# Down projection of 16 of the 22 f tiles as block products with sums in HBM, and the FFN in the order of a list scheduler

## The chip, the cores and the metric

The kernel runs on one core of one Trainium2 chip. A core has a matrix engine (PE in the profile), a vector engine (DVE), a scalar engine (ACT), GpSimd (POOL) and SyncE (SP), and 16 DMA engines that move data between HBM and the on-chip memory SBUF. The matrix engine adds up into PSUM, which this kernel uses as 8 banks of 128x512 fp32. The metric is the device time of one launch in microseconds (us), lower is better.

## The reference

One hybrid decoder layer on 1024 tokens of width 1024, in fp32: a mixer (attention and short convolution), then a gated ConvFFN. The change touches the FFN alone:

```python
h = rms_norm(x, norm_ffn_pre[l])
u = causal_dwconv(h @ w_up[l], conv_ffn_w[l])
a, g = jnp.split(u, 2, axis=-1)
f = (jax.nn.gelu(g, approximate=True) * a) @ w_down[l]
x = x + rms_norm(f, norm_ffn_post[l])
```

`w_up` is 1024 x 5632, `w_down` is 2816 x 1024. The 2816 FFN channels are 22 f tiles of 128 channels.

## The kernel before

**Numbers.** Every fp32 operand of a matmul is scaled by a power of two and split into two f16 tensors, hi and lo: ACT writes hi (L97), DVE writes lo as the rest (L98). A product is then three f16 matmuls, hi by hi, hi by lo and lo by hi (`PASSES`). The power of two comes from the sum of squares of the operand: ACT squares a tile and sums (L58), PE adds over partitions (L76), DVE builds the scale. All matmuls of the FFN put 512 columns through the array.

**Up projection.** For each f tile the channels a and g are computed as a 2x2 block product with seven products instead of eight (Strassen's scheme): class `Up`, `prod` (L1594), 12 matmuls a product, 84 an f tile. The products are evicted by ACT (L1609) or DVE (additions), then each of a and g goes through a three-tap convolution (one ACT pass L1669, two DVE passes L1671), g through gelu on ACT (L1678), and DVE multiplies (L1679): the result `ua` is an f tile, channels by tokens, 128x1024 fp32. `pair_fetch`, `pair_sums` and `pair_split` load `w_up`, form the sums of weight blocks that the scheme needs and split them.

**Down projection.** The f tiles are taken in groups, `GROUPS = (2, 4, 4, 4, 4, 4)`. `f_split` splits a group's f tiles, `dn_split` loads its `w_down` tiles (L1331) and splits them; `dn_sums` had loaded the same tiles earlier (L1269) for their sums of squares. `down` goes over 8 token tiles of 128 and 2 halves of 512 outputs, each 4 f tiles by 3 passes, 12 matmuls into one bank (L1368). The bank is evicted at once: for the first group by ACT into the accumulator `yacc` (L1373), for the others by DVE, which multiplies by the scale and adds to `yacc` in SBUF (L1375). Per group of four that is 192 matmuls and 16 evictions. The last group also takes the norm of each token row, scales it and sends it out: seven token tiles by a DMA of POOL that adds into `out` in HBM (L1388), the last by SP (L1393).

**Order.** The loop at the end of `ffn` writes the f tiles in turn; the `down` of group g-1 stands in the middle of group g, behind the second f tile's `prod(3)`. Each engine's own order is set by the tile framework's scheduler, from its own priorities. Buffers come from rings: 16 slabs of 128x1024 fp32 (`slot`), 4 for raw weights (`ws`), 8 for split weights (`wh`), 4 and 4 for the accumulators (`o16`, `x`), 8 PSUM banks.

Of the kernel before, what the change touches and what calls it, by code (L numbers as in the profile page):

```python
# [16 lines left out]
F16 = mybir.dt.float16  # L17
# [7 lines left out]
P = 128  # L25
# [9 lines left out]
GROUPS = (2, 4, 4, 4, 4, 4)  # L35
# [4 lines left out]
class Layer:  # L40
# [234 lines left out]
    def mixer(self, mid):  # L275
# [884 lines left out]
        dram = self.top.enter_context(tc.tile_pool(name="dram", bufs=1, space=bass.MemoryType.DRAM))  # L1160
# [112 lines left out]
    dpos, dsums, pz = 0, {}, None  # L1273

# [35 lines left out]
    def ffn(self):  # L1310
# [27 lines left out]
        def down(g, between=None):  # L1338
# [7 lines left out]
            for tt in range(8):  # L1346
                if between:
                    between(tt)
                if g == 0:
                    yacc[tt] = (self.o16p.tile([P, D], F32, tag="o16", name=f"yacc{tt}") if tt < 4 else  # L1350
                                self.xp.tile([P, D], F32, tag="x", name=f"yacc{tt}"))
# [18 lines left out]
                for nh, part in enumerate(parts):  # L1370
                    ps, sl = pd[nh], ds(*part)
                    if g == 0:
                        nc.scalar.activation(y[:, sl], ps, AF.Copy, scale=sm[:, 0:1])  # L1373
                    else:
                        nc.vector.scalar_tensor_tensor(y[:, sl], ps, sm[:, 0:1], y[:, sl], ALU.mult, ALU.add)  # L1375
# [27 lines left out]
        for g in range(ng):  # L1403
            for n in range(GROUPS[g]):
                f = ff0[g] + n
                p = prs[f]
                begun = n == 2 and 1 <= g < ng - 1
                if f >= 1 and not begun:
                    if f >= 2:
                        p.prod(1)  # L1410
                    prs[f - 1].prod(4)
                if f >= 1 and f + 1 < NFF:
                    self.pair_split(f"u{f + 1}")
                if 1 <= f and f + 2 < NFF:
# [309 lines left out]
```

## Time and profile before

| what | us |
|---|---|
| median of 3 runs | 1332.78 (1332.39 to 1333.75) |
| profiled execution, its own time | 1334.14 |
| its span | 1332.4 |
| PE, DVE, ACT, POOL busy in the span | 1313.9, 1049.9, 858.9, 34.4 |
| down projection's matmuls (L1368), 1068 records | 230.3 |

The span runs from the first to the last recorded instruction; the execution's own time is longer by 1.74 us. The FFN takes about the last 650 us of the span, from 682 on. An engine's busy time counts its instructions' own durations; matmuls are pipelined, so a busy PE says only that PE was never without work. Rows by group give a line of the kernel, engine, operation, tiles, shapes and count, then the busy total, the mean of one in ns, and the time for which the engine stood idle just before them and what ended it. Rows by stretch give, for each engine, the busy time in a window, then the clock that TensorE was granted (1.00 is full), the mean busy share of the 16 DMA engines and GB/s.

### The profile page before, as it was taken

How to read it: one execution, taken by the hardware profiler on the slowest of the kernel's cores; microseconds unless marked ns; L12 is line 12 of the kernel's file. 1: busy time of each engine (PE TensorE's matmuls, PEld its weight loads, DVE VectorE, ACT ScalarE, POOL GpSimd, SP SyncE). 2: the span in 40 equal slices, each digit the busy share in tenths (PEclk: the TensorE clock that was granted, in tenths of full speed). 3: DMA queues.
4: the chain of work that ended last, by engine and by line, in shares of the span. 5: the costliest groups of instructions: out<-in, count | busy, mean ns of one | idle time of the engine just before them, and what ended most of it. 6: DMA issues, size and time to landing. Idle time of an engine off the chain costs nothing.

```text
span 1332.4 us, 16830 instructions
## 1 busy us (share of the span) xinstructions
PE 1313.9 (99%) x6505; PEld 590.3 (44%) x6505; DVE 1049.9 (79%) x1701; ACT 858.9 (64%) x1210; POOL 34.4 (3%) x58
## 2 busy tenths in 40 slices
PE   8999999999999999999999999999999999999997
PEld 4444444444444444444444444444444444444443
DVE  6578988887888967877898968966994895798855
ACT  6578878787878966566574877625751762576424
POOL 2000000000000000000110000000000000000002
PEclk9999999999999999999999999999999999999999
DMA  7101210111102112332431113223130321312126
GB/s 270 33 33 33 63 32 32 33 33 32 49 0 67 60 52 91 114 139 63 145 107 34 48 48 127 63 64 121 41 92 26 116 67 46 126 47 111 64 48 111
DMA packets 26610, 96.12 MB, mean 72 GB/s; under 512 B 3089, under 2 KB 3217, under 8 KB 26530
## 3 DMA queue, kind: packets, MB, share of 16 engines
q1 hardware_dynamic: 25088, 89.80, 20.7%
q0 software_dynamic: 1440, 5.24, 2.1%
q8 instruction: 51, 0.84, 0.3%
q14 instruction: 29, 0.24, 0.1%
q10 hardware_dynamic: 2, 0.00, 0.0%
HBM read 86.62 MB, written 8.42 MB: 71 GB/s over the span
## 4 chain that ended last, share of the span: by engine, by line
PE 89%; DVE 6%; ACT 2%; DMA 1%; issue 1%; POOL 0%; SPq 0%; POOLq 0%; DVEq 0%; ACTq 0%
PE pd L1368 16%; PE py L1179 5%; PE pcb L211 3%; PE pcc L211 3%; PE pcx L211 3%; PE pk L211 3%; PE pq L211 3%; PE pywa L805 3%; PE pywc L805 3%; PE A L833 2%; PE o L833 2%; PE z L833 2%; PE pv L406 1%; PE pv L444 1%; PE pga L211 1%
## 5 line engine op out<-in xcount | busy, mean ns | idle before, releaser
L1594 PEld LDWEIGHTS <-wh_u 128*128 128x128 f16 x1848 | 178.8, 98 | 215.1 <-issue 1.2
L1368 PE MATMUL pd<-wdh,f 128*128 128x512 f16 (+1 forms) x1068 | 230.3, 377 | 2.3 <-ACT wdh L97 1.7
L1368 PEld LDWEIGHTS <-f 128*128 128x128 f16 x1068 | 104.4, 98 | 126.5 <-issue 3.6
L97 ACT ACTIVATE wh_u<-ws_u,sc 128x1024 f16<-128x1024 f32 (+1 forms) x66 | 64.7, 999 | 98.3 <-DVE sc L80 79.4
L1375 DVE SCALAR_TENSOR_TENSOR yacc<-pd,sd,yacc 128x512 f32<-128x512 f32 (+1 forms) x81 | 58.6, 741 | 72.7 <-PE pd L1368 65.2
L1594 PEld LDWEIGHTS <-wh_g 128*128 128x128 f16 x588 | 56.9, 98 | 68.6 <-issue 0.2
L1179 PE MATMUL py<-wh_wo,m 128*128 128x512 f16 x384 | 83.7, 379 | 0.0
L98 DVE SCALAR_TENSOR_TENSOR wh_u<-ws_u,sc,wh_u 128x1024 f16<-128x1024 f32 (+1 forms) x66 | 72.2, 1101 | 10.7 <-ACT wh_u L97 10.6
L876 ACT ACTIVATE sh<-sp 128x1024 f16<-128x1024 f32 (+3 forms) x48 | 40.4, 842 | 52.3 <-DVE sp L871 52.1
L1671 DVE SCALAR_TENSOR_TENSOR ugu<-cgu,cw_g,ugu 128x1023 f32<-128x1023 f32 (+1 forms) x44 | 56.3, 1279 | 10.1 <-ACT ugu L1669 9.6
L871 DVE TENSOR_TENSOR sp<-A,sp 1x1024 f32<-1x1024 f32 (+3 forms) x40 | 35.9, 897 | 29.9 <-PE A L833 26.5
L1671 DVE SCALAR_TENSOR_TENSOR ua<-cau,cw_a,ua 128x1023 f32<-128x1023 f32 (+1 forms) x44 | 56.2, 1278 | 1.4 <-ACT ua L1669 1.3
L1179 PEld LDWEIGHTS <-m 128*128 128x128 f16 x384 | 37.4, 98 | 44.2
L880 DVE TENSOR_TENSOR sh<-sp,sh 128x1024 f16<-128x1024 f32 (+3 forms) x48 | 45.8, 954 | 13.5 <-ACT sh L876 13.3
L906 DVE SCALAR_TENSOR_TENSOR w<-e,w 128x1024 f16<-128x1024 f32 (+3 forms) x48 | 45.8, 953 | 6.8 <-ACT w L902 6.7
L902 ACT ACTIVATE w<-e 128x1024 f16<-128x1024 f32 (+3 forms) x48 | 40.5, 843 | 14.8 <-DVE e L897 13.7
L897 DVE TENSOR_TENSOR e<-e,g 128x1024 f32<-128x1024 f32 (+3 forms) x48 | 45.7, 952 | 2.5 <-ACT g L893 2.5
L866 ACT ACTIVATE sp<-e,one 128x1024 f32<-128x1024 f32 (+3 forms) x48 | 44.4, 925 | 4.0 <-DVE e L861 2.7
L58 ACT ACTIVATE jk_u<-ws_u 128x1024 bf16<-128x1024 f32 x44 | 46.4, 1054 | 0.8 <-DMA ws_u<-w_up_nt 0.2
L852 ACT ACTIVATE e<-z,cz 128x1024 f32<-128x1024 f32 (+3 forms) x48 | 43.0, 897 | 3.6 <-PE z L833 3.6
L211 PE MATMUL pcb<-hT,wh_cb 128*128 128x512 f16 x192 | 45.1, 380 | 0.0
L211 PE MATMUL pcx<-hT,wh_cx 128*128 128x512 f16 x192 | 44.9, 379 | 0.0
(711 smaller groups left out, 2625.8 us busy)
## 6 DMA issues: line engine op xcount, KB each, us to landing
ws_u<-w_up_nt SPq DMA_DIRECT2D x44, 512.0 KB
ds<-w_down SPq DMA_DIRECT2D x22, 512.0 KB
wd<-w_down SPq DMA_DIRECT2D x22, 512.0 KB
ws_g<-w_in_nt SPq DMA_DIRECT2D x14, 512.0 KB
x<-x SPq DMA_DIRECT2D x8, 512.0 KB
ws_wo<-w_out SPq DMA_DIRECT2D x8, 512.0 KB
xr<-x SPq DMA_DIRECT2D x8, 512.0 KB
out<-x SPq DMA_DIRECT2D x7, 512.0 KB
```

Source lines behind the costliest of these rows:

```text
L58: self.nc.scalar.activation(self.junk(f"jk_{name}"), src, AF.Square, accum_out=acc)
L97: self.nc.scalar.activation(dst[:, 0, :], src, AF.Copy, scale=s)
L98: self.nc.vector.scalar_tensor_tensor(dst[:, 1, :], src, s, dst[:, 0, :], ALU.mult, ALU.subtract)
L211: nc.tensor.matmul(ps, w[:, wi, ds(k * P, P)], hT[:, hi, k, ds(c * NH, NH)], start=n == 0, stop=n == last)
L805: nc.tensor.matmul(ps, w[0][:, wi, ds((d % 2) * NH + k * P, P)], acts[bi][k][:, hi, ds(c * NH, NH)], start=n == 0, stop=n == 11)
L833: nc.tensor.matmul(out, w, mv, skip_group_check=True, **kw)
L880: nc.vector.tensor_tensor(sh[:, 1, :, off:], u["sp"][:, :, off:], sh[:, 0, :, off:], ALU.subtract)
L1179: nc.tensor.matmul(ps, m16[k][:, hi, ds(tt * P, P)], wo[k][:, wi, sl], start=k == 0 and p == 0, stop=k == 7 and p == 2)
L1368: nc.tensor.matmul(pd[nh], f16[g][k][:, hi, ds(tt * P, P)], w[k][:, wi, ds(*part)], start=run is runs[0] and n == 0, stop=run is runs[-1] ...
L1375: nc.vector.scalar_tensor_tensor(y[:, sl], ps, sm[:, 0:1], y[:, sl], ALU.mult, ALU.add)
L1594: nc.tensor.matmul(ps, w[wt][:, wi, ds(wc * NH + k * P, P)], self.block(i, hi, k), start=first and n == 0, stop=n == 3 * KH - 1, skip_grou ...
L1671: nc.vector.scalar_tensor_tensor(u[:, lag:], c[:, :T - lag], sm[:, 2 - lag:3 - lag], u[:, lag:], ALU.mult, ALU.add)
```

## The change

`GROUPS` becomes (4, 4, 4, 4, 3, 3), and the first `NQ = 4` groups, 16 f tiles, are no longer multiplied as 4 x 16 plain blocks but as "quads". A quad takes its four f tiles as two pairs (x, y) and cuts tokens and outputs in halves, so that each pair is a 2x2 by 2x2 block product, and writes it as seven products `OPS` in the order 1, 2, 5, 3, 7, 4, 6. A product is 4 token tiles by (2 pairs x 3 passes), 24 matmuls; 168 a quad where `down` had 192.

- **Operands.** `f_quads` and `w_quads` form the block sums (`comb`, DVE, 128x512 fp32, 8 for f and 8 for w) and split them: for f and for w each six full splits of 128x1024 and two half ones of 128x512, where four full ones stood for each.
- **Eviction.** After each product ACT scales the bank into a slab tile `st` (28 times a quad, 128x512); two banks fill one tile. Products 2, 3 and 4 go on adding in the banks of 1, 5 and 7 after those were evicted, so the scheme's own sums are partly made in PSUM.
- **Sums in HBM.** Each `st` (512 KB) goes by a DMA of POOL to one of 14 tensors `acc` in HBM: 14 a quad, written plainly by the first quad and added there (`accum_op`) by the other three. At the end of quad 3, `join` builds the eight `yacc` tiles: 20 loads of 256 KB on SP, 8 adding loads of 256 KB on POOL, 12 additions of 128x512 on DVE.
- **The rest.** The last two groups of three f tiles are multiplied by `down` as before, evicted by DVE (16 and 17 evictions). `w_down` is loaded once for quads 1 to 3, twice for quad 0 and for the last six tiles: 32 loads instead of 44. `dn_sums` in the mixer now covers four tiles instead of two.
- **Order.** From the first `prod` after the mixer to the last group, what PE, DVE, ACT, SP and POOL do is registered as jobs of a class `Plan`, with a cost for each kind (the table `C`), a limit on how far ahead of its need a job may run (`AHEAD`), due times (`DUE`) and the sizes of the buffer rings. `Plan.order` runs the list through a model of the engines; the instructions are then written in that order under a manual schedule. PE's matmuls keep the order in which they are written; the other engines take the ready job whose need is nearest. The model lets one DMA after another pass: an `st` has mb=1.6 there, adding or not, a load of 512 KB mb=1.3 (`load`). The tail (`down` of the last two groups) is left to the framework's scheduler.

Lines in the listings of the changed kernel are its own. ACT around the `down` of group 1, before (`f16` and `wdh` are split f and `w_down`, `jk` the squares, `ua` and `ugu` convolution and gelu, `cgu` an eviction of the up projection):

```order
L97 ACTIVATE f16_1_2_7819<-ua4_7356,sc27_7804 128x1024
L97 ACTIVATE f16_1_3_7822<-ua5_7521,sc27_7804 128x1024
L97 ACTIVATE wdh_1_0_7836<-wd2_1_0_7834,sc28_7825 128x1024
L97 ACTIVATE wdh_1_1_7841<-wd2_1_1_7839,sc28_7825 128x1024
L58 ACTIVATE jk_f6_7746,sm_f2_6591<-ua6_7669 128x1024
L1669 ACTIVATE ugu7_7775<-cgu7_7693,cw_g7_7902 128x1024
L97 ACTIVATE wdh_1_2_7846<-wd2_1_2_7844,sc28_7825 128x1024
L97 ACTIVATE wdh_1_3_7851<-wd2_1_3_7849,sc28_7825 128x1024
L1669 ACTIVATE ua7_7867<-cau7_7692,cw_a7_7868 128x1024
L1609 ACTIVATE cgu8_7887<-pu8a_7873 128x512
L1678 ACTIVATE ugu7_7775<-ugu7_7775 128x1024
L58 ACTIVATE jk_f7_7909,sm_f2_6591<-ua7_7867 128x1024
L58 ACTIVATE jk_u10_0_8166,sm_u10_8163<-ws_u10_0_8164 128x1024
L58 ACTIVATE jk_u10_1_8170,sm_u10_8163<-ws_u10_1_8168 128x1024
```

ACT around product 1 of quad 1, after (`fx`, `fs` are split f sums, `wq` split w sums, `st` the evictions of the banks `pq`):

```order
L1462 ACTIVATE fx_1_0_8338<-ua4_7252,sp_f1_8184 128x1024
L1701 ACTIVATE st1_1_0_8370<-pq1_0_1_8322,sd1_8239 128x512
L1701 ACTIVATE st1_1_0_8370<-pq1_1_1_8331,sd1_8239 128x512
L1701 ACTIVATE st1_1_2_8374<-pq1_2_1_8342,sd1_8239 128x512
L1462 ACTIVATE fs_1_0_8378<-ua5_7489,sp_f1_8184 128x1024
L1701 ACTIVATE st1_1_2_8374<-pq1_3_1_8350,sd1_8239 128x512
L59 ACTIVATE jk_f8_8389,sm_f2_6599<-ua8_8193 128x1024
L1462 ACTIVATE fs_1_1_8400<-ua7_8054,sp_f1_8184 128x1024
L1462 ACTIVATE fx_1_1_8411<-ua6_7904,sp_f1_8184 128x1024
L1569 ACTIVATE ua9_8420<-ca9_8258,cw_a9_8030 128x1024
L1569 ACTIVATE ug9_8281<-cg9_8209,cw_g9_8408 128x1024
L1462 ACTIVATE wq_1_5_8432<-ds5_7804,sp_dn1_7882 128x1024
```

The evictions now stand on ACT between splits, convolution passes and gelus, where before it had no eviction of the down projection after the first group.

DVE in the `down` of group 1, before:

```order
L1679 TENSOR_TENSOR ua7_7867<-ugu7_7775,ua7_7867 128x1024
L1375 SCALAR_TENSOR_TENSOR yacc0_7116<-pd1_0_0_7913,sd1_7911,yacc0_7116 128x512
L1375 SCALAR_TENSOR_TENSOR yacc0_7116<-pd1_0_1_7914,sd1_7911,yacc0_7116 128x512
L1375 SCALAR_TENSOR_TENSOR yacc1_7133<-pd1_1_0_7941,sd1_7911,yacc1_7133 128x512
L1375 SCALAR_TENSOR_TENSOR yacc1_7133<-pd1_1_1_7942,sd1_7911,yacc1_7133 128x512
L1668 TENSOR_SCALAR cw_a8_8242<-cfw_91,sc26_7708,g_ffn_5681 128x3
L1375 SCALAR_TENSOR_TENSOR yacc2_7150<-pd1_2_0_7969,sd1_7911,yacc2_7150 128x512
L1375 SCALAR_TENSOR_TENSOR yacc2_7150<-pd1_2_1_7970,sd1_7911,yacc2_7150 128x512
```

DVE ahead of quad 1, after (L1464 is the lo half of a split, L1469 a `comb`, L1543 an eviction of the up projection):

```order
L1571 SCALAR_TENSOR_TENSOR ug8_8124<-cg8_8068,cw_g8_7815,ug8_8124 128x1022
L1469 TENSOR_TENSOR ua5_7489<-ua4_7252,ua5_7489 128x512
L1543 TENSOR_TENSOR cg9_8209<-pu9b_8219,cg9_8209 128x512
L1469 TENSOR_TENSOR ua7_8054<-ua6_7904,ua7_8054 128x512
L1469 TENSOR_TENSOR ua4_7252<-ua4_7252 128x512
L1469 TENSOR_TENSOR ua6_7904<-ua6_7904 128x512
L1469 TENSOR_TENSOR ua4_7252<-ua5_7489,ua4_7252 128x512
L1469 TENSOR_TENSOR ua6_7904<-ua7_8054,ua6_7904 128x512
L1469 TENSOR_TENSOR ua5_7489<-ua5_7489,ua4_7252 128x512
L1469 TENSOR_TENSOR ua7_8054<-ua7_8054,ua6_7904 128x512
```

DVE no longer adds banks to `yacc` there; it makes the block sums of f in place, and the splits of these sums wait for them.

POOL between the mixer and the tail, before:

```order
L182 TENSOR_TENSOR r_post7_6370<-r_post7_6370,neghalf_86 128x1
L182 TENSOR_TENSOR r_ffn7_6433<-r_ffn7_6433,neghalf_86 128x1
L1345 DMA g_ffn_post_11097<-g_ffn_post 128x1024
L182 TENSOR_TENSOR fin0_11100<-fin0_11100,neghalf_86 128x1
L1388 DMA out<-o0_11099 128x1024
```

POOL at the end of quad 3, after (`acc5_0` is product 5's sum for the first two token tiles):

```order
L1428 DMA acc7_0_6615<-st3_7_0_10417 128x1024
L1428 DMA acc7_1_6616<-st3_7_2_10451 128x1024
L1428 DMA acc4_0_6609<-st3_4_0_10507 128x1024
L1428 DMA acc4_1_6610<-st3_4_2_10522 128x1024
L1428 DMA acc6_0_6613<-st3_6_0_10535 128x1024
L1428 DMA acc6_1_6614<-st3_6_2_10559 128x1024
L1428 DMA yacc4_10509<-acc5_0_6611 128x512
L1428 DMA yacc5_10512<-acc5_0_6611 128x512
L1428 DMA u2_0_10262<-acc6_0_6613 128x512
```

Where POOL had nothing to do through the FFN, it now issues the transfers of all quads in turn, and the adding loads of `join` stand behind quad 3's last ones.

```diff
-GROUPS = (2, 4, 4, 4, 4, 4)
+GROUPS = (4, 4, 4, 4, 3, 3)
+NQ = 4
...
                     if last:
                         nc.scalar.activation(self.junk(f"jf{tt}_{nh}")[:, sl], y[:, sl], AF.Square,
                                              accum_out=sm_[:, 3 + nh:4 + nh])
@@ -1400,49 +1396,517 @@
             g = max(g for g in range(ng) if ff0[g] <= f)
             fts[g].append(prs[f].finish(smfs[g][:, f - ff0[g]:f - ff0[g] + 1]))
 
...
-        for g in range(ng):
+        lo, hi = ds(0, NH), ds(NH, NH)
+        pl = Plan(dict(s=16, ws=4, wh=8, o16=4, x=4, pm=8))
+        C = dict(A=0.97, Ah=0.5, Aq=1.18, V=1.21, Vh=0.64, Vp=0.72)
...
+        def load(eng, b, dst, srcf, mb=1.3, r=(), w=None, **kw):
+            e = nc.sync if eng == "SP" else nc.gpsimd
+            j = pl.add(eng, 0.45 if eng == "SP" else 1.1, lambda: e.dma_start(dst(), srcf(), **kw), r,
+                       [b] if w is None else w, ahead=1e9 if kw or r else AHEAD["load"])
...
+        def comb(o, oc, x, xc, y, yc, op, **kw):
+            V(C["Vh"], lambda: vec.tensor_tensor(o.t[:, oc], x.t[:, xc], y.t[:, yc], op),
+              [(x, "l" if xc is lo else "h"), (y, "l" if yc is lo else "h")], [(o, "l" if oc is lo else "h")], **kw)
+
+        AHEAD = dict(load=45.0, sq=40.0, up=32.0, quad=40.0, wq=60.0)
...
+        def f_quads(g):
+            sb = fb[g] = f_scale(g, 1)
+            q = up[f"q{g}"] = Pr()
...
+            q.a11 = slab(f"fa_{g}", [P, 2, T], F16)
+            for p in range(2):
+                halves(q.a11, ds(p * NH, NH), xs[p], lo, sb, n=NH, dreg=f"{p}", sreg="l", ahead=ah)
...
+            for p in range(2):
+                halves(q.ya[p], fall, ys[p], fall, sb, ahead=ah)
+            for p in range(2):
+                x, y = xs[p], ys[p]
+                comb(y, hi, x, hi, y, hi, ALU.add, ahead=ah)
+                comb(x, hi, x, lo, x, hi, ALU.subtract, ahead=ah)
+                comb(x, lo, y, hi, x, lo, ALU.subtract, ahead=ah)
+                comb(y, lo, y, lo, x, lo, ALU.subtract, ahead=ah)
+            for p in range(2):
+                halves(q.ys[p], fall, ys[p], fall, sb, ahead=ah)
+            for p in range(2):
+                halves(q.xs[p], fall, xs[p], fall, sb, ahead=ah)
...
+                load("SP", b, lambda b=b: b.t, lambda n=n: a["w_down"][ff0[g] + n])
+                A(C["Aq"], lambda n=n, b=b: self.sumsq(b.t, sq.t[:, n:n + 1], f"dn{ff0[g] + n}"), [b], [sq], ahead=AHEAD["wq"])
...
+        def w_quads(g):
...
+                sq.tile = self.dsums[g]
+                raw = [slab(f"wr_{g}_{n}") for n in range(4)]
+                for n, b in enumerate(raw):
+                    load("SP", b, lambda b=b: b.t, lambda n=n: a["w_down"][ff0[g] + n])
...
+            for p in range(2):
+                halves(q.b11, ds(p * NH, NH), xs[p], lo, sb, n=NH, dreg=f"{p}", sreg="l", ahead=ah)
+            for p in range(2):
+                halves(q.yb[p], fall, ys[p], fall, sb, ahead=ah)
+            for p in range(2):
+                x, y = xs[p], ys[p]
+                comb(x, lo, x, hi, x, lo, ALU.subtract, ahead=ah)
+                comb(x, hi, y, hi, x, hi, ALU.subtract, ahead=ah)
+                comb(y, hi, y, hi, x, lo, ALU.subtract, ahead=ah)
+                comb(y, lo, y, lo, y, hi, ALU.subtract, ahead=ah)
+            for p in range(2):
+                halves(q.xt[p], fall, xs[p], fall, sb, ahead=ah)
+            for p in range(2):
+                halves(q.yt[p], fall, ys[p], fall, sb, ahead=ah)
...
+        acc, accb = {}, {}
+        for i in range(1, 8):
+            for e in range(2):
+                acc[i, e] = self.dram.tile([P, 2, NH], F32, tag=f"acc{i}_{e}", name=f"acc{i}_{e}")
+                accb[i, e] = note()
+        OPS = {1: ("a11", None, "b11", None), 2: ("ya", 0, "yb", 0), 3: ("ys", 0, "yb", 1), 4: ("ya", 1, "yt", 0),
+               5: ("ys", 1, "xt", 0), 6: ("xs", 0, "yt", 1), 7: ("xs", 1, "xt", 1)}
...
+        def quad_prod(g, i):
+            q, w = up[f"q{g}"], up[f"w{g}"]
+            ft, fc, wt_, wc = OPS[i]
...
+            for tt in range(4):
+                if first:
+                    q.ps[tt] = Buf("pm", lambda tt=tt: self.bank(f"pq{g}_{tt}_{i}"))
...
+                if tt % 2 == 0:
+                    st = slab(f"st{g}_{i}_{tt}", [P, 2, NH])
+
...
+                    for p in range(2):
+                        fo, wo = p if fc is None else fc, p if wc is None else wc
+                        for h, x in PASSES:
+                            pe.matmul(b.t, fa[p].t[:, h, ds(fo * NH + tt * P, P)], wa[p].t[:, x, ds(wo * NH, NH)],
+                                      start=first and n == 0, stop=n == 5, skip_group_check=True)
+                            n += 1
+                pl.add("PE", 1.3, mm, fa + wa, [b], seq=True)
+                A(C["Ah"], lambda tt=tt, b=b, st=st: act.activation(st.t[:, tt % 2, :], b.t, AF.Copy, scale=q.sd.t[:, 0:1]),
+                  [b, q.sd], [(st, str(tt % 2))])
+                if tt % 2:
+                    kw = {} if g == 0 else dict(accum_op=ALU.add)
+                    load("G", None, lambda e=tt // 2: acc[i, e], lambda st=st: st.t, r=[st], w=[accb[i, tt // 2]], mb=1.6, **kw)
...
+        def join(tt):
+            y = yb_[tt] = Buf("o16", lambda: self.o16p.tile([P, D], F32, tag="o16", name=f"yacc{tt}"))
+            z = yb_[tt + 4] = Buf("x", lambda: self.xp.tile([P, D], F32, tag="x", name=f"yacc{tt + 4}"))
+            u = slab(f"u2_{tt}", [P, NH])
+
...
+            def ld(eng, b, sl, reg, i, **kw):
+                load(eng, None, lambda: b.t[:, sl], lambda: m(i), r=[accb[i, tt // 2]], w=[(b, reg)], mb=0.65, **kw)
+            ld("SP", u, slice(0, NH), None, 1)
+            ld("SP", z, lo, "l", 4)
+            ld("SP", z, hi, "h", 7)
+            ld("SP", y, lo, "l", 2)
+            ld("SP", y, hi, "h", 3)
+            ld("G", u, slice(0, NH), None, 6, accum_op=ALU.add)
+            ld("G", z, hi, "h", 5, accum_op=ALU.add)
+            for b, sl, reg in ((y, hi, "h"), (z, lo, "l"), (z, hi, "h")):
+                V(C["Vh"], lambda b=b, sl=sl: vec.tensor_tensor(b.t[:, sl], b.t[:, sl], u.t, ALU.add), [u], [(b, reg)])
...
+            for f in range(NFF):
+                g = max(g for g in range(ng) if ff0[g] <= f)
...
+                if f >= 1 and not (n == 2 and 1 <= g <= NQ):
+                    up_prod(f - 1, 4)
+                    up_done(f - 1)
+                if n == 0 and 1 <= g <= NQ:
+                    f_quads(g - 1)
...
+                if f + 3 < NFF:
+                    up_weights(f + 3)
+                if n == 1 and 1 <= g <= NQ:
+                    quad_open(g - 1)
+                    for k, i in enumerate((1, 2, 5, 3, 7, 4, 6)):
+                        quad_prod(g - 1, i)
+                        if k == 0:
+                            up_prod(f, 4)
+                            up_done(f)
+                if n == 1 and g < NQ:
+                    w_quads(g)
+                if n == 1 and g >= NQ:
+                    w_sums(g)
+                if g == NQ and n == 2:
+                    for tt in range(4):
+                        join(tt)
...
+        while todo:
+            best = None
+            for e, now in eng.items():
+                c = ready[e]
+                if e == "PE" and pos < len(seq) and not seq[pos].n:
+                    c = c + [seq[pos]]
+                pick = None
+                for j in c:
+                    t = max(now, j.t0, j.late - j.ahead)
+                    for b in j.bufs:
+                        if b.pool and not b.begun:
+                            t = max(t, free[b.pool][0] if free[b.pool] else 1e9)
+                    key = (max(t, now + 0.05), j.late - (100 if e == "PE" and not j.seq else 0))
+                    if t < 1e8 and (pick is None or key < pick[0]):
+                        pick = key, t, j
+                if pick and (best is None or pick[1] < best[0]):
+                    best = pick[1], e, pick[2]
...
+            end = t + j.cost
+            eng[e] = end
+            done = end + j.lag
+            if e in ("SP", "G"):
+                dma = max(dma, t + 0.8) + j.load
+                done = max(done, dma + 1.2)
```

More of the change, by code (lines that the diff above doesn't have):

```diff
@@ L1273 @@
     dpos, dsums, pz = 0, {}, None
+    ahead_set, due_set = {}, {}
     def bank(self, name):
@@ L1371, in down @@
                     ps, sl = pd[nh], ds(*part)
[L1372 to L1375, printed above, removed]
+                    nc.vector.scalar_tensor_tensor(y[:, sl], ps, sm[:, 0:1], y[:, sl], ALU.mult, ALU.add)
                     if last:
@@ L1440, in ffn @@
+        self.pw[f"u{NFF - 1}"] = [b.t for b in p.w], pr.inv
         dn_split(ng - 2)
```

347 lines of the change are left out of this document (310 added, 37 removed).

## The prediction

> **What bounds the kernel now.** I read the busy times first, then the chain of work that ended last, both on the page of the kernel before.
>
> ```profile
> span 1332.4 us, 16830 instructions
> PE 1313.9 (99%) x6505; PEld 590.3 (44%) x6505; DVE 1049.9 (79%) x1701; ACT 858.9 (64%) x1210; POOL 34.4 (3%) x58
> PE 89%; DVE 6%; ACT 2%; DMA 1%; issue 1%; POOL 0%; SPq 0%; POOLq 0%; DVEq 0%; ACTq 0%
> ```
>
> PE is busy for 99% of the span and makes 89% of the chain. Next, what PE waits for in the FFN (us in total, times, longest):
>
> ```profile
> PE pd L1368 <- ACT wdh L97: 1.7, 3, 0.8
> PE pt L1197 <- DVE hn L1189: 1.1, 1, 1.1
> PE pu0a L1594 <- ACT cgu L1609: 0.7, 1, 0.7
> PE pd L1368 <- DVE wdh L98: 0.6, 1, 0.6
> ```
>
> Those are all of its waits there, 4.1 us in 650. So matmuls taken away come off the time, as long as nothing else becomes late. How near the others are is told by stretches: a part of the mixer, the first FFN stretch, one group's period each in the third and fourth row, the tail, a dense part of the fourth row's period, and the last wait of the kernel.
>
> ```profile
> 500.00:600.00 100.00, 100.00 (x470) 45.34 (x469) 77.45 (x134) 62.63 (x93) 1.30 (x2) 1.00 0.34 114
> 682.00:793.00 111.00, 108.72 (x515) 49.79 (x513) 93.33 (x152) 74.58 (x111) 3.61 (x4) 1.00 0.18 57
> 906.80:1022.30 115.50, 115.50 (x543) 52.39 (x540) 88.74 (x135) 61.24 (x81) 0.00 (x0) 1.00 0.23 73
> 1137.20:1242.30 105.10, 104.66 (x491) 47.41 (x490) 91.55 (x145) 71.51 (x97) 0.00 (x0) 1.00 0.26 91
> 1242.30:1332.40 90.10, 83.10 (x397) 38.67 (x396) 58.94 (x92) 34.23 (x56) 11.24 (x16) 0.97 0.39 82
> 1170.00:1230.00 60.00, 60.00 (x283) 27.20 (x282) 58.01 (x89) 42.10 (x55) 0.00 (x0) 1.00 0.26 88
> 1324.20:1329.50 5.30, 1.23 (x12) 0.85 (x9) 3.57 (x9) 1.53 (x6) 1.44 (x2) 0.81 0.69 112
> ```
>
> The columns are window, length, then busy time of PE, PEld, DVE, ACT and POOL, the granted clock, the DMA share and GB/s. In a group's period (906.8 to 1022.3) PE never stands, DVE is busy 77%, ACT 53%.
>
> **The sum, PE.** One stretch of the chain prices the matmul:
>
> ```profile
> 883.50 23.31 PE pd L1368 x108
> ```
>
> 23.31 / 108 = 0.2158 us. Each of four quads has 168 matmuls for 192, so 96 fewer: -20.7 us. The last six f tiles keep theirs. That the instructions are really fewer, the order of the built kernel shows; nothing is left of a rival by which the change doesn't do what it says.
>
> **DVE and ACT work of a quad.** The rows, by shape over the whole run, and the plain evictions in one period:
>
> ```profile
> L97 ACT ACTIVATE f<-ua,sc 128x1024 f16<-128x1024 f32 x22 | 23.5, 1134 | 9.3 <-DVE sc L80 9.3
> L98 DVE SCALAR_TENSOR_TENSOR f<-ua,sc,f 128x1024 f16<-128x1024 f32 x22 | 27.5, 1277 | 1.0 <-ACT f L97 1.0
> L97 ACT ACTIVATE wh_u<-ws_u,sc 128x512 f16<-128x512 f32 x22 | 15.7, 714 | 10.0 <-DVE ws_u L1304 9.7
> L98 DVE SCALAR_TENSOR_TENSOR wh_u<-ws_u,sc,wh_u 128x512 f16<-128x512 f32 x22 | 16.4, 745 | 0.1
> L1290 DVE TENSOR_TENSOR s_u<-s_u,ws_u 128x512 f32<-128x512 f32 x22 | 15.1, 686 | 0.2
> L1373 ACT ACTIVATE yacc<-pd,sd 128x512 f32<-128x512 f32 x16 | 10.4, 718 | 5.8 <-PE pd L1368 5.2 <-PE pr L76 0.6
> L1375 DVE SCALAR_TENSOR_TENSOR yacc<-pd,sd,yacc 128x512 f32<-128x512 f32 x16 | 11.5, 748 | 16.5 <-PE pd L1368 14.7 <-PE pr L76 1.8
> ```
>
> For f and w together a quad has 4 full and 4 half splits more, 16 block sums more, 28 evictions on ACT, and loses 16 on DVE.
>
> DVE: 88.74 + 4 x 1.277 + 4 x 0.745 + 16 x 0.686 - 16 x 0.748 = 95.8 us. The period shrinks from 115.5 to 110.3 (24 matmuls), so DVE stands at 87%. ACT: 61.24 + 4 x 1.134 + 4 x 0.714 + 28 x 0.718 = 88.7 us, 80%.
>
> Is that tolerable? The stretch 1137.2 to 1242.3 had DVE at 87% with PE idle for 0.44 us, and in 1170 to 1230 DVE was 97% busy and PE never idle. So load alone is no bound. What counts is waiting in line. In the old period DVE was idle 26.8 us, 16.5 of it ahead of the evictions that now go; the other 10.3 may stay: 95.8 + 10.3 = 106.1 of 110.3, it fits with 4.2 us over.
>
> ACT is where a new wait can arise. Products 2, 3 and 4 add in the banks of 1, 5 and 7, which ACT must have evicted. Between 5 and 3, and 7 and 4, the first bank has three groups of six matmuls, 3.9 us, until it is wanted again. ACT with two full splits ahead of the eviction needs 2 x 1.134 + 0.718 = 3.0 us: in time; with three, 4.1: late by 0.2. Behind such an eviction on ACT stand the next splits, so lateness there is passed on to DVE's lo halves and to PE. The lower end is 0 (88.7 fits in 110.3). For the upper end I take two further full splits ahead of each of three bank pairs in four quads, 12 x 2 = 24 us. I take 1 us a quad, **4 us**, near the low end, since the trace shows PE at rest under DVE loads as high.
>
> **Transfers.** Adding transfers from POOL are in the trace only in the tail, between 1294 and 1324.2; beside them a group's loads, in the period from 906.8 to 1022.3:
>
> ```profile
> q0 software_dynamic: 864, 3.15, 68.8%
> out<-o POOLq DMA_DIRECT2D x6, 512.0 KB, 5.4
> ...
> q1 hardware_dynamic: 2304, 8.39, 22.9%
> ```
>
> 68.8% of 30.2 us for 6 transfers is 3.46 us of all 16 engines for each, and 5.4 us from issue to landing. A load: 22.9% of 115.5 us for 16 (8.39 MB of 512 KB each), 1.65 us. A quad issues 14 transfers while PE does 168 + 12 matmuls, 38.8 us. At 3.46 us they need 48.4 us, and the last is 9.6 us behind. Quad 0 writes plainly, near the load's 1.65: 23 us, no backlog.
>
> Who waits for a landing? The slab is in a ring of 16. In the order of the changed kernel the slab of a quad's first `st` is taken again, by an ACT split of the same quad, some 4.3 us of matmuls later, so 1.1 us too early; slabs from the middle of a quad come 6.5 to 16 us later. ACT then waits with all its evictions behind it. In quad 3 `join` and the last `w_down` loads want slabs too, and I count 4 to 10 us. I take 1 us for quads 1 and 2 together and 4 for quad 3: **5 us**, between 0 and, with all three quads as bad as the worst of quad 3's count, 30.
>
> The Trainium skill, page "DMA: Bandwidth & Descriptors", section "Anatomy of one DMA — SWDGE (gpsimd) path", gives a POOL transfer about 2.0 us fixed plus its bytes at 436 GB/s; for 512 KB that moves in 1.2 us, 14 of them in 16.8, and by it this term would be 0 and the forecast 5 us lower. The trace's adding transfers took nearly three times that, and I go by the trace.
>
> **Join, tail, front.** `join` moves 20 x 0.83 us of loads and 8 x 1.73 of adding ones (halves of the sizes above), 30 us of the DMA engines, while PE works on the last up projections; its 12 additions are 8.2 us of DVE. `w_up` loads for the last f tiles stand behind the loads on SP, with some 40 us of matmuls as cover; if that goes, 30 us of DMA time is at risk, which is in the upper end above. In the tail the last `down` has 18 matmuls a token tile, 3.9 us, where the adding output needs 3.46: it keeps up, barely. PE idles 7.0 us in the old tail. I add **1 us**, between 0 and 2. Two sums of squares more in the mixer hide under ACT's 63% there: 0. POOL:
>
> ```profile
> POOL g_ffn_post L1345 <- DVE f L98: 572.9, 1, 572.9
> L1388 POOL DMA_DIRECT2D out<-o x7: 874/879/926, 1293.8 to 1324.4; - x7
> ```
>
> 64 issues at 0.88 us are 56 us, on an engine that stood idle 572.9 us in one piece: 0. The 12 loads of `w_down` that go free 20 us of DMA time (12 x 1.65), which no one waited for: 0.
>
> Sum: -20.7 + 4 + 5 + 1 = -10.7. The profiled execution took 1334.1 us, 1.36 over the median of the runs shown; 1334.1 - 10.7 = 1323.4, less 1.4 gives **1322.0 us**. Its own range, by stalls between 5 and 17 us in place of 10, is 1317 to 1329.
>
> **Rivals.**
>
> *All hidden.* Adding transfers next to other work pass as fast as loads, 14 x 1.65 = 23 us under 38.8, and ACT is always in time. For it: PE's 4.1 us of waits. Against: 3.46 us is measured. Stalls up to 3 us: 1312 to 1315.
>
> *Transfers back up.* The 3.46 us was measured with POOL's transfers alone; beside loads each may take half as long again, 5.2 us. Then a quad's last is 14 x 5.2 - 38.8 = 34 us behind, the order's margin is at most 16, and 18 us are lost in each of three quads: 1312 + 5 + 54 = 1371. It decides where a loss of (20.7 - 5) / 3 = 5.2 us a quad eats the gain, at a backlog of 21.2 us, that is 4.3 us a transfer. Against: DMA is at 23% in a period, and 12 fewer loads come.
>
> *ACT in line becomes the bound.* The upper end of that term, 24 us in place of 4: 1342. It decides at 14.7 us, 1.2 us for each of the 12 bank pairs. For it: 28 evictions in a fixed order between 1.1 us instructions. Against: 20% of ACT stays free.
>
> *The clock falls.* The row 1324.2 to 1329.5 has the clock at 0.81 with PE waiting, all rows with waits of up to 1.1 us have 1.00. If the stalls come as long waits, each adds 5.3 x 0.19 = 1.0 us of slow matmuls; two a quad or so make 4 to 8 us more: 1326 to 1330. The Trainium skill, "TensorE: Matmul & The Clock Gate", Part 1 on the HAM clock gate, has the clock at half after an idle window of about 3.4 us; by that only the wait in quad 3 would matter, and the trace so far agrees.
>
> **How the numbers follow.** The forecast 0.45, all hidden 0.20, transfers back up 0.10, ACT in line 0.15, clock 0.10. The measurement tells about 0.2% from no change, 2.7 us: faster is below 1330.1, slower above 1335.4. Faster: 0.45 + 0.20 and a little over half of the clock's, 0.70. Slower: 0.10, and most of 0.15: 0.23. Same: 0.07. The range reaches from just under the hidden case, 1310, to 1340, and leaves out the backed-up transfers and the upper third of the ACT case, and some 0.03 below.
>
> **What would show it.** The count of down matmuls and their duration show the -20.7. PE's waits in the quads: on ACT's `st` evictions (my 4 us), on split f or w late because a slab's transfer had not landed (my 5 us, most of it in quad 3). The busy share of POOL's queue divided by 14 gives the time of an adding transfer; well under 3 us is the hidden case, over 4.3 the backlog. DVE near 96 and ACT near 89 us a period confirm the loads; if DVE waits longer than 10 us for ACT's halves, the fit of 106 in 110 fails. A granted clock under 1.00 in the FFN is the clock's case. Most wrong I would be if the list scheduler's order lets PE wait for a split in every f tile, in the up projection too, which I priced at nothing: the row 682 to 793 shows 2.3 us idle there under ACT at 67%, and the planned order moves every one of these instructions.

## The result: 1354.5 us, slower by 1.6%

The changed kernel takes 1354.53 us (median of 4 runs, 1353.41 to 1355.78), the kernel before beside it 1333.22 us. The ratio is 1.0161, interval 1.0143 to 1.0178: 21 us slower, where 11 us faster was forecast. The page of the changed kernel:

```profile
span 1351.8 us, 17009 instructions
...
PE 1302.7 (96%) x6406; PEld 582.3 (43%) x6406; DVE 1095.4 (81%) x1761; ACT 942.0 (70%) x1338; POOL 85.7 (6%) x122
```

PE's own work has gone down by 11 us (1302.7 for 1313.9) and the span has grown by 19. What PE waits for in the FFN, the first rows:

```profile
PE pr_u L1450 <- DVE rb_u L1441: 15.3, 3, 10.0
PE pq L1697 <- ACT st L1701: 5.8, 5, 3.0
PE pr_u L1450 <- ACT st L1701: 3.3, 1, 3.3
```

`pr_u` is a small thing: the matmul with one column that adds the squares of a `w_up` tile over the partitions, for the scale of weights that are wanted later. PE takes its work in order, so nothing written behind `pr_u` starts while it waits. `rb_u` (the sums that `pr_u` reads) is late because ACT's squares are late, and these because of a load. Behind the longest wait the next product was held up too: ACT evicted the bank that it goes on adding in only at 1210.01, in line behind the same squares. ACT's waits from 780 to 1260, where all quads lie:

```profile
ACT jk_u L59 <- DMA ws_u<-w_up_nt: 29.4, 10, 12.9
ACT jk_dn L59 <- DMA ds<-w_down: 15.0, 9, 2.8
...
ACT ug L1550 <- DMA acc<-st: 6.2, 1, 6.2
...
ACT st L1701 <- DMA acc<-st: 3.3, 3, 2.6
...
ACT fx L1462 <- DMA acc<-st: 3.0, 2, 1.6
...
ACT fs L1462 <- DMA acc<-st: 2.5, 1, 2.5
```

44.4 us on loads of `w_up` and `w_down` (`jk` are the squares of just loaded tiles), 15.0 us on slabs whose transfer had not landed (`acc<-st`). Not all of it is new or does harm: with no transfers in quads 1 to 3 (run 2 below) the two rows of loads still sum to 14.6 us there, the slab rows are gone, and PE waits 2.1 us in all. The same by stretches: quad 0, which writes plainly, quads 1, 2 and 3, and one piece of the last (columns as in the prediction).

```profile
818.00:860.00 42.00, 42.00 (x198) 19.05 (x197) 31.52 (x56) 36.70 (x57) 6.40 (x12) 1.00 0.67 251
920.00:980.00 60.00, 53.84 (x244) 23.64 (x243) 38.22 (x64) 44.02 (x65) 11.49 (x14) 0.97 0.84 193
1040.00:1100.00 60.00, 52.86 (x247) 23.53 (x245) 36.77 (x64) 43.48 (x66) 10.24 (x12) 1.00 0.80 187
1155.00:1235.00 80.00, 65.90 (x284) 28.46 (x283) 47.45 (x74) 49.13 (x72) 19.00 (x22) 0.89 0.98 246
1200.00:1220.00 20.00, 9.98 (x35) 3.76 (x33) 5.83 (x14) 6.50 (x11) 7.90 (x9) 0.66 1.06 318
```

Beside quad 0 PE never stands. Beside quads 1 and 2 the DMA engines move less, 193 and 187 GB/s for 251, yet they are busy for 84% and 80% where it was 67%, and PE stands for 6 to 7 us in each. From 1200 on they are full (1.06), and the clock is at 0.66. The price of a transfer, plain beside quad 0 (818 to 860) and adding beside quad 1 (920 to 975):

```profile
q0 software_dynamic: 1728, 6.29, 39.1%
...
acc<-st POOLq DMA_DIRECT2D x12, 512.0 KB, 3.9
```

```profile
q0 software_dynamic: 2015, 7.34, 70.3%
q1 hardware_dynamic: 1001, 3.65, 18.2%
...
acc<-st POOLq DMA_DIRECT2D x14, 512.0 KB, 11.2
```

39.1% of 42 us for 12 plain ones is 1.37 us each; 70.3% of 55 us for 14 adding ones is 2.76 us. Adding doubles the time on the 16 DMA engines, and the time to landing goes from 3.9 to 11.2 us. How that reaches PE, behind quad 2, on ACT and on PE (start, length, instruction, and in brackets what it waited for):

```profile
1072.64 1.06 ACT L59 ACTIVATE jk_u<-ws_u 128x1024 bf16<-128x1024 f32 x1 [4.13 <-DMA ws_u<-w_up_nt]
...
1076.43 1.06 ACT L59 ACTIVATE jk_u<-ws_u 128x1024 bf16<-128x1024 f32 x1 [2.07 <-DMA ws_u<-w_up_nt]
...
1080.25 1.06 ACT L59 ACTIVATE jk_dn<-ds 128x1024 bf16<-128x1024 f32 x1 [0.94 <-DMA ds<-w_down]
...
1083.54 1.06 ACT L59 ACTIVATE jk_dn<-ds 128x1024 bf16<-128x1024 f32 x1 [1.66 <-DMA ds<-w_down]
...
1087.43 1.06 ACT L59 ACTIVATE jk_dn<-ds 128x1024 bf16<-128x1024 f32 x1 [2.75 <-DMA ds<-w_down]
...
1088.49 0.58 ACT L1550 ACTIVATE ug<-pu14c 128x512 f32<-128x512 f32 x1
...
1091.18 1.06 ACT L59 ACTIVATE jk_dn<-ds 128x1024 bf16<-128x1024 f32 x1 [1.07 <-DMA ds<-w_down]
```

```profile
1078.78 0.18 PE L1450 MATMUL pr_u<-rb_u,ones 128*128 128x1 bf16 x1 [3.29 <-ACT st L1701]
...
1089.12 2.75 PE L1537 MATMUL pu14c<-hA,wh_u 128*128 128x512 f16 x12 [1.84 <-ACT ug L1550]
```

ACT stands six times for a load, with evictions in line behind it: the `st` that frees PE's bank, and `ug<-pu14c`, which ran at 1088.49 although its product had long been there. The four `ds` tiles come 3.3 to 3.9 us apart; in the kernel before a load held the engines for 1.65 us.

### The profile page after: what moved, and what is told of

It reads as the page before. It is cut to its first block, busy times and chain, and to the rows that moved or that the text cites. A ratio compares the mean times of both kernels' runs of the same rounds, so it can differ in the third digit from the quotient of the medians.

```text
span 1351.8 us, 17009 instructions
## 1 busy us (share of the span) xinstructions
PE 1302.7 (96%) x6406; PEld 582.3 (43%) x6406; DVE 1095.4 (81%) x1761; ACT 942.0 (70%) x1338; POOL 85.7 (6%) x122
## 4 chain that ended last, share of the span: by engine, by line
PE 49%; issue 25%; DVE 11%; DMA 6%; ACT 5%; POOL 4%; POOLq 0%; DVEq 0%; SPq 0%; ACTq 0%
PE py L1180 5%; PE pcb L212 3%; PE pcc L212 3%; PE pcx L212 3%; PE pk L212 3%; PE pq L212 3%; PE pywa L806 3%; PE pywc L806 3%; DMA ws_u<-w_up_nt 3%; PE pd L1367 3%; POOL acc L1428 2%; PE A L834 2%; PE o L834 2%; PE z L834 2%; PE pv L407 1%
## 5 line engine op out<-in xcount | busy, mean ns | idle before, releaser
L1537 PEld LDWEIGHTS <-wh_u 128*128 128x128 f16 x1764 | 172.0, 98 | 216.2 <-issue 13.1
L1464 DVE SCALAR_TENSOR_TENSOR wh_u<-ws_u,sc_u,wh_u 128x1024 f16<-128x1024 f32 (+1 forms) x60 | 65.6, 1104 | 28.0 <-ACT wh_u L1462 27.7
L1701 ACT ACTIVATE st<-pq,sd 128x512 f32<-128x512 f32 x112 | 70.0, 686 | 19.9 <-DVE ua L1582 13.3
L1428 POOL DMA_DIRECT2D acc<-st x56 | 43.4, 774 | 466.9 <-ACT st L1701 466.9
L1367 PE MATMUL pd<-wdh,f 128*128 128x512 f16 (+1 forms) x297 | 62.4, 372 | 0.6 <-ACT wdh L98 0.6
L1462 ACT ACTIVATE wh_u<-ws_u,sc_u 128x1024 f16<-128x1024 f32 (+1 forms) x60 | 59.3, 998 | 3.8 <-DVE sc_u L1447 3.5
L881 DVE TENSOR_TENSOR sh<-sp,sh 128x1024 f16<-128x1024 f32 (+3 forms) x48 | 45.8, 955 | 13.5 <-ACT sh L877 13.3
L1571 DVE SCALAR_TENSOR_TENSOR ua<-ca,cw_a,ua 128x1023 f32<-128x1023 f32 (+1 forms) x40 | 51.1, 1278 | 1.1 <-ACT ua L1569 1.1
L1697 PE MATMUL pq<-wq,fs 128*128 128x512 f16 x192 | 44.6, 389 | 5.0 <-ACT st L1701 4.7
L1571 DVE SCALAR_TENSOR_TENSOR ug<-cg,cw_g,ug 128x1023 f32<-128x1023 f32 (+1 forms) x38 | 48.6, 1278 | 0.0
L867 ACT ACTIVATE sp<-e,one 128x1024 f32<-128x1024 f32 (+3 forms) x48 | 44.4, 926 | 4.0 <-DVE e L862 2.7
```

Of the source, the lines that this page charges most:

```text
L1367: nc.tensor.matmul(pd[nh], f16[g][k][:, hi, ds(tt * P, P)], w[k][:, wi, ds(*part)], start=run is runs[0] and n == 0, stop=run is runs[-1] ...
L1428: j = pl.add(eng, 0.45 if eng == "SP" else 1.1, lambda: e.dma_start(dst(), srcf(), **kw), r, [b] if w is None else w, ahead=1e9 if kw or r ...
L1462: A(C["A" if big else "Ah"], lambda: act.activation(dst.t[:, 0, dsl], src.t[:, ssl], AF.Copy, scale=sb.t["s"]), [(src, sreg), sb], [(dst, ...
L1464: V(C["V" if big else "Vh"], lambda: vec.scalar_tensor_tensor(dst.t[:, 1, dsl], src.t[:, ssl], sb.t["s"], dst.t[:, 0, dsl], ALU.mult, ALU. ...
L1537: pe.matmul(b.t, p.w[wt].t[:, wi, ds(wc * NH + k * P, P)], pr.block(i, h, k), start=first and n == 0, stop=n == 3 * KH - 1, skip_group_che ...
L1571: V(C["V"], lambda lag=lag: vec.scalar_tensor_tensor(u.t[:, lag:], c.t[:, :T - lag], sm.t[:, 2 - lag:3 - lag], u.t[:, lag:], ALU.mult, ALU ...
```

## The experiments

Theory A after this look: the adding transfers hold the DMA engines, loads land late, ACT's order has work on these loads ahead of evictions, and PE stands. Rival B: the planned order keeps PE waiting by itself. Rival C: fourteen transfers in a quad are too many, adding or not. Medians of 4 runs (10 for the scheduler alone), the kernel before beside each at 1333.1 to 1333.6 us.

**1. Plain writes.** The sums over the quads are left out.

```diff
-                    kw = {} if g == 0 else dict(accum_op=ALU.add)
+                    kw = {}
```

> Quads 1 to 3 write their 42 tiles plainly to HBM, as quad 0 does, in place of adding; every instruction stays in its place. Left out: the sums over the quads. Theory A (adding holds the 16 DMA engines 2.76 us a transfer against 1.37 us of quad 0's plain ones, so loads land late and ACT, which takes its work in order, stands): PE's waits in quads 1 to 3 go nearly to quad 0's, which were nil, with the two clock drops there; 1318 to 1332 us. Rival B (the planned order keeps PE waiting, whatever the transfers): within 10 us of 1354. Rival C (14 transfers of any kind in a quad are too many): above 1340.

1324.55 us (1323.99 to 1325.53), ratio 0.9937 (0.9923 to 0.9952). Same order, as many transfers of the same size, 30 us less. In quads 1 and 2 PE never stands:

```profile
920.00:980.00 60.00, 60.00 (x284) 27.27 (x283) 47.82 (x79) 49.18 (x72) 6.91 (x13) 1.00 0.51 193
1040.00:1100.00 60.00, 60.00 (x284) 27.27 (x283) 47.67 (x83) 47.86 (x70) 5.84 (x11) 1.00 0.52 193
1155.00:1235.00 80.00, 73.14 (x333) 32.59 (x332) 57.02 (x95) 53.28 (x77) 11.22 (x16) 0.96 0.69 225
```

B and C fall for the quads. What is left lies in the last row, beside `join`: one wait of PE of 6.4 us and a clock of 0.96.

**2. No transfers in quads 1 to 3.** The sums over the quads are left out here too.

```diff
+ jb.fn = (lambda: None) if g else jb.fn
```

> The 42 transfers of quads 1 to 3 are not issued; the rest stays in its place. Left out: the sums over the quads. Theory A: up to 10 us under the run with plain writes, 1312 to 1325. Rival B: above 1345. Rival C: 1312 to 1325 too, but with the plain writes above 1340.

1316.19 us (1314.99 to 1316.89), ratio 0.9876 (0.9859 to 0.9892). PE's busy time from 680 to the end, before and here:

```profile
680.00:1333.00 653.00, 641.34 (x3015) 292.38 (x3013) 511.31 (x796) 362.92 (x505) 14.84 (x20) 1.00 0.25 75
```

```profile
680.00:1314.00 634.00, 619.49 (x2909) 282.10 (x2906) 555.52 (x854) 441.68 (x627) 30.09 (x42) 1.00 0.29 88
```

641.3 to 619.5: the whole saving of the matmuls, with 28 evictions a quad more on ACT beside it. So the transfers cost 1354.5 - 1316.2 = 38.3 us, and the rest of the change gains 17.

**3. The planner told the price.** Same work, another order.

```diff
-..., mb=1.6, **kw)
+..., mb=1.6 if g == 0 else 2.76, **kw)
```

> The list scheduler is told 2.76 us for an adding transfer in place of 1.6, nothing else; same work in another order. If the loss is the plan's wrong price (its order puts work on ACT that waits for loads which it takes to be there), the order heals most of it: 1325 to 1340. If the DMA engines are simply too full in a quad (14 x 2.76 = 38.6 us and 8 loads beside 38.8 us of matmuls), it heals less than half: 1340 to 1352. Rival B: no change beyond 5 us.

1341.18 us (1339.61 to 1345.91), ratio 1.0067 (1.0048 to 1.0087): 13.3 us of the 38 come back. That is less than half, and the time lies just inside the second range, 1340 to 1352. The rows tell it by place:

```profile
920.00:980.00 60.00, 58.70 (x274) 26.37 (x273) 44.23 (x69) 46.52 (x68) 11.10 (x14) 1.00 0.83 193
1040.00:1100.00 60.00, 58.11 (x272) 26.04 (x271) 43.60 (x72) 47.00 (x71) 10.22 (x12) 1.00 0.76 186
1155.00:1235.00 80.00, 69.51 (x319) 30.62 (x318) 46.67 (x83) 48.71 (x73) 16.37 (x19) 1.00 0.94 240
```

Beside quads 1 and 2 the DMA engines are busy for 83% and 76%, hardly less than before, yet PE stands for 1.3 and 1.9 us where it was 6.2 and 7.1. So the occupation itself is not the loss there; an order that takes a load to be there is. In the last row PE still stands for 10.5 of 80 us (14.1 in the changed kernel): there the price heals only a part.

**4. The scheduler alone.** The four groups are multiplied plainly, in the planner's order, with the accumulators in SBUF. The core of the edit:

```diff
-                    for k, i in enumerate((1, 2, 5, 3, 7, 4, 6)):
-                        quad_prod(g - 1, i)
-                        if k == 0:
-                            up_prod(f, 4)
-                            up_done(f)
+                    up_prod(f, 4)
+                    up_done(f)
+                    p_down(g - 1)
```

> The list scheduler without the block products: the four groups are multiplied plainly, 192 matmuls each, evicted into the accumulators in SBUF as in the kernel before, groups (4, 4, 4, 4, 3, 3), all in the planner's order. Theory A: the planned order itself costs nothing, 1322 to 1336. Rival B: the planned order loses by itself, above 1345.

1334.23 us, ratio 1.0011 (1.0001 to 1.0020): 1 us slower, at most some 2.7. With plain products the planned order neither gains nor loses more than that by itself; for the order of the quads run 2 says the same. The fear at the end of the prediction, waits of PE in every f tile, did not come true.

**5. Join late.**

```diff
-..., w=[(b, reg)], mb=0.65, **kw)
+..., w=[(b, reg)], mb=0.65, **kw).ahead = 20.0
```

> One number: the transfers of join may start no earlier than 20 us (in the plan's time) ahead of their need, so they no longer stand on SP ahead of the w_up loads of f tiles 20 and 21. If the 10.0 us wait of PE at 1201 us and the clock at half behind it (13.7 us long, 6.8 us lost) come from join on SP's queue: 1354 - 17 = 1338, 1334 to 1344. If these loads are late because of the adding transfers alone: above 1349.

1341.41 us (1341.03 to 1342.05), ratio 1.0062 (1.0047 to 1.0077): 13.1 us, a little less than the 17 expected. The road is not quite the one I had written. In the changed kernel, the chain in order of time, and a row each of ACT and PE:

```profile
1187.74 2.84 DVE wh_u L1464 x3
1190.59 16.74 DMA ws_u<-w_up_nt
...
1214.00 20.46 DMA ws_u<-w_up_nt
```

```profile
1207.35 1.06 ACT L59 ACTIVATE jk_u<-ws_u 128x1024 bf16<-128x1024 f32 x1 [12.90 <-DMA ws_u<-w_up_nt]
```

```profile
1211.14 0.18 PE L1450 MATMUL pr_u<-rb_u,ones 128*128 128x1 bf16 x1 [10.02 <-DVE rb_u L1441]
```

By the chain the first of these `w_up` loads left SP as soon as DVE's split had freed its buffer, so it did not stand on SP behind `join`. But it took 16.74 us to land, in DMA engines full of quad 3's adding transfers and of loads of `join`, six of which SP had issued from 1184.28 on, just ahead of it. From 1190 to 1208:

```profile
q0 software_dynamic: 666, 2.40, 66.8%
q1 hardware_dynamic: 1093, 2.52, 38.4%
...
yacc<-acc SPq DMA_DIRECT2D x8, 256.0 KB
```

ACT stood for 12.9 us, PE for 10.0, and then the clock fell. The next load on the chain took 20.46 us, but no wait of PE followed it. With `join` late, the loads for the same `pr_u` left SP at 1184.69, and the first one's squares began 8.1 us later:

```profile
1184.69 0.99 SPq L1428 DMA_DIRECT2D ws_u<-w_up_nt  x2
...
1192.83 1.06 ACT L59 ACTIVATE jk_u<-ws_u 128x1024 bf16<-128x1024 f32 x1 [4.45 <-DMA ws_u<-w_up_nt]
```

Whether `join` delays the load by its share of the engines or by standing ahead of it in the same DMA queue, no run separates.

The last quad's stretch is mostly healed (76.22 of 80 us for PE, where it was 65.90), quads 1 and 2 are as they were:

```profile
920.00:980.00 60.00, 53.73 (x245) 23.66 (x244) 38.70 (x66) 44.52 (x66) 11.92 (x14) 0.97 0.84 193
1040.00:1100.00 60.00, 54.14 (x243) 23.61 (x241) 35.64 (x60) 42.47 (x63) 10.22 (x12) 0.97 0.82 190
1155.00:1235.00 80.00, 76.22 (x352) 34.16 (x350) 60.55 (x99) 60.60 (x87) 18.99 (x22) 0.98 0.96 242
```

**6. Both.** The price of run 3, and in `join` a third edit beside run 5's: its adding loads, too, are told about twice the price.

```diff
-..., mb=0.65, **kw)
+..., mb=1.38 if kw else 0.65, **kw).ahead = 20.0
```

> The price told (2.76 us) and join late together; whole work, its order alone differs. If the two are separate causes: the 13 us of the told price and the most part of join's 17 add up, 1326 to 1333. If the told price had already healed join: 1338 to 1343.

1325.27 us (1322.02 to 1327.83), ratio 0.9939 (0.9921 to 0.9956): 29.3 us under the changed kernel, a little more than the sum of 13.3 and 13.1, and 0.7 us under the range for two separate causes. How much of that is the third edit is open. Two causes: the price in quads 1 to 3, and `join`'s transfers beside the last of them.

**7. The quad split.** As run 6, with products 7 and 4 an f tile later.

```diff
-                    for k, i in enumerate((1, 2, 5, 3, 7, 4, 6)):
+                    for k, i in enumerate((1, 2, 5, 3, 6)):
...
+                if n == 2 and 1 <= g <= NQ:
+                    for i in (7, 4):
+                        quad_prod(g - 1, i)
```

> As the run before it in this call, but products 7 and 4 of each quad are done an f tile later, behind 84 more matmuls of the up projection (18 us): 10 adding transfers, 27.6 us of the DMA engines, in the 28.5 us of the first five products, and 4 in the rest. If crowding in time is the cause, and not the number of bytes: 1315 to 1325, faster than both kernels. If holding the f and w operands longer starves the slabs: above 1333.

1319.49 us (1318.87 to 1319.78), ratio 0.9895 (0.9879 to 0.9912): the whole computation, 1.05% faster than the kernel before, and 3.3 us over the run without the transfers.

```profile
920.00:980.00 60.00, 60.00 (x284) 27.30 (x283) 46.87 (x81) 49.94 (x74) 11.43 (x14) 1.00 0.89 193
1040.00:1100.00 60.00, 60.00 (x283) 27.23 (x282) 48.20 (x79) 47.28 (x69) 8.55 (x10) 1.00 0.83 191
1155.00:1235.00 80.00, 80.00 (x376) 36.35 (x375) 63.51 (x101) 54.97 (x78) 13.78 (x16) 1.00 0.93 247
```

PE is busy in all of these 200 us, with the DMA engines at 83 to 93%.

**8. Half the transfers.** Of each product in quads 1 to 3, the transfer of the last two token tiles is left out, with its part of the sums.

```diff
-..., mb=1.6, **kw)
+..., mb=1.6, **kw).skip = g > 0 and tt == 3
```

> Of the 42 adding transfers of quads 1 to 3 only those of the first two token tiles of each product are issued, 21; everything else stays in its place. Left out: the sums over the quads for the other two token tiles. Crowding (a threshold): 7 x 2.76 + 8 loads x 1.4 = 30.5 us fit beside 38.8 us of matmuls, so quads 1 and 2 lose under 2 us each, 1318 to 1328. If each transfer costs by itself (0.9 us each, 38 us over 42): 1335.

1322.99 us (1320.71 to 1324.41), ratio 0.9921 (0.9907 to 0.9936). Half of the transfers cost 6.8 us over none, the other half 31.5. So there is no fixed price per transfer; a threshold between 7 and 14 a quad fits. Of the 6.8 us a wait of 4.6 us lies beside `join`.

**9. Written twice.** Plain writes, each tile to two places; the sums over the quads are left out.

```diff
-..., mb=1.6, **kw)
+..., mb=1.6, **kw).again = (lambda e=tt // 2, i=i, st=st: nc.gpsimd.dma_start(acc2[i, e], st.t)) if g else None
```

> The run with plain writes, but quads 1 to 3 write each tile twice, to two places in HBM: 28 plain transfers a quad, 28 x 1.37 = 38.4 us of the DMA engines, as much as 14 adding ones; twice the bytes. Left out: the sums over the quads. If the time on the DMA engines is the cause: 1345 to 1360, as the changed kernel. If adding does harm in some other way (its own latency, its reads of HBM): near the plain writes' 1324.6, under 1335.

1347.12 us (1345.63 to 1348.42), ratio 1.0103 (1.0088 to 1.0118), 22.6 us over the plain writes.

POOL's queue beside quad 1 (920 to 975):

```profile
q0 software_dynamic: 4003, 14.56, 69.4%
```

69.4% where the changed kernel had 70.3%: no adding, twice the bytes, as much time on the engines, and 22.6 of the 30 us are back. The time on the engines is what this run and the changed kernel share, so it harms without any addition; the other 7 us are not explained by it.

**10. The split alone**, with the old price and the early `join`.

> Products 7 and 4 an f tile later, as in the fastest run, but with the planner's old price (1.6 us) and join as the change has it. If spreading the transfers is what heals the quads: their 14 us of waits go and join's 13 to 17 us stay, 1332 to 1340. If the planner must know the price, spreading heals little: above 1345. If spreading does all, join too: under 1328.

1347.51 us (1345.01 to 1350.79), ratio 1.0113 (1.0092 to 1.0133). The time lies where the second expectation has it, above 1345, but its reason does not hold for quads 1 and 2.

```profile
920.00:980.00 60.00, 59.79 (x282) 27.08 (x281) 46.54 (x81) 49.80 (x74) 11.42 (x14) 1.00 0.90 193
1040.00:1100.00 60.00, 60.00 (x284) 27.22 (x282) 48.63 (x79) 47.80 (x70) 9.19 (x11) 1.00 0.86 193
1155.00:1235.00 80.00, 62.07 (x265) 26.66 (x264) 42.86 (x66) 42.89 (x65) 15.66 (x18) 0.91 0.87 214
```

Quads 1 and 2 are healed without the price (59.79 and 60.00 of 60). But in the last row 62.07 of 80 us is worse than the changed kernel's 65.90. The chain there:

```profile
1171.71 12.26 DMA ws_u<-w_up_nt
```

A `w_up` load takes 12.26 us: `join`, with no limit on how early it may start, still begins beside quad 3 (its first loads leave SP at 1143.74), whose last products now come later. Spreading the transfers and telling the price are two cures for the same trouble in quads 1 and 2. That `join` needs its own is what the last row points to; no run has the split with `join` late and the old price.

## Why the prediction was wrong

**PE, -20.7 us: right.** Run 2 shows it in full, 21.8 us of busy time.

**DVE and ACT, 4 us: right in kind, too high.** Without the transfers PE waits 2.1 us in all from 780 to 1260, at any place. That is hardly more than in the kernel before (1.8 us idle in that stretch). 28 evictions a quad on ACT and the splits do no harm by themselves; the rival "ACT in line" did not arise without late loads.

**The transfers, 5 us with 30 as the upper end: this is the step that failed.** They cost 38.3 us: PE's waits from 780 to 1260 are 28.5 us for 2.1 without them, and the slower clock takes 9.7 more. The sum asked "who waits for a landing?", and answered with the slabs alone. ACT's waits for slabs are there, 15.0 us. What I left out is that `w_up` and `w_down` loads use the same 16 engines. I had both prices in hand, 48.4 us of transfers beside 38.8 us of matmuls, and 23% for the loads, and drew the backlog for the transfers' own buffers only. The loads' cover was never priced, and on ACT the work on them stands ahead of the evictions: 44.4 us of waits, where 14.6 remain without the transfers. 18.6 of PE's 28.5 us are waits at `pr_u`, which needs the squares of loads; how the rest divides between late loads and late slabs no run separates. I also took 3.46 us from the tail's adding transfers into `out`; those of the quads take 2.76. Why the two differ is open: in the changed kernel's own tail they still take 3.4. The error in the price went the other way from the error in the sum.

**The rival "transfers back up"** had the right cause, at a chance of 0.10, and the wrong road: it put the loss on slabs, beyond a margin of 16 us, and gave 1371. Its break-even of 4.3 us a transfer was wrong too: 2.76 was enough. The point is whether loads still land in time for the order, and run 8 shows that beside 7 transfers a quad they do.

**Join: named, and costed at nothing.** The prediction saw that `w_up` loads stand behind it on SP and counted 40 us of matmuls as cover. It was not a wait on SP that counted: `join` came on top of quad 3's adding transfers, and a load that took 16.7 us to land used the cover up. It is worth 13 us (run 5).

**The clock, as a rival:** it came on top of the waits, and larger than priced. PE's busy time from 680 on is 629.2 us, against 619.5 in run 2 with the same matmuls: 9.7 us at a slower clock, most of it behind the one wait of 10.0 us. I had 1.0 us a long wait.

```profile
680.00:1352.00 672.00, 629.23 (x2917) 283.78 (x2915) 556.50 (x857) 443.34 (x629) 66.12 (x84) 0.98 0.44 116
```

**No backlog, by the rate of the Trainium skill:** the page that the prediction cites, "DMA: Bandwidth & Descriptors", section "Anatomy of one DMA — SWDGE (gpsimd) path", would have had this term at 0. Run 1 shows what that is worth: the rate comes near the plain writes (1.37 us in the trace, 1.2 as an estimate by that rate), and with those the change would have been faster. It does not hold for the adding ones, 2.76 us.

**Tail and front, 1 and 0 us:** a little low. From PE's last matmul to the end it is 9.7 us for 7.0 before, 2.7 more where 0 to 2 was allowed (0.9 more in run 2), and in the first FFN stretch (700 to 780) PE stands 1.4 us longer than before.

## What to carry to other kernels

Where a change adds transfers, list what else uses the DMA engines in the same stretch, loads first, and ask which engine takes the late load's work in order and what is queued behind it. A planner that sets a fixed order turns a wrong price into waits: here 1.6 for 2.76 us cost 13 us, with the same transfers. Before giving up a scheme whose compute saving is real, spread its transfers, tell the planner their price, and hold transfers that nobody needs yet until the crowded stretch is over: together these made 1354.5 into 1319.5 us.

## What the runs showed of the hardware

An adding transfer from SBUF to HBM takes twice a plain one's time on the DMA engines, 2.76 for 1.37 us at 512 KB; in the tail of the kernel before it was 3.46. The Trainium skill, page "DMA: Bandwidth & Descriptors", section "Anatomy of one DMA — SWDGE (gpsimd) path", has one rate for POOL's transfers and does not set adding ones apart; the measurement decides.

The DMA engines can be busy for 93% of 80 us without a wait of PE (run 7), and at 84% cost 6 us of 60 (the changed kernel). The share alone says little.

After the wait of 10.0 us the clock was 0.66 in the mean over 1200 to 1220. The first twelve matmuls behind it took 5.28 us, twelve at 1219.29 took 2.75, so it had fallen to about half; with half and full alone, 0.66 is 20 x 0.34 / 0.5 = 13.6 us at half. That an idle window halves the clock the Trainium skill says too ("TensorE: Matmul & The Clock Gate", Part 1 on the HAM clock gate), and these rows agree; the prediction's own row, 0.81 in the tail, had made it 1 us a wait.
